# Block loads and accumulating additions pinned to program order on GpSimd's queue, the next set's first block asked for at product 2, gate halves spilled one set later

## The chip, the cores and the metric

The kernel runs on one core of a Trainium2 chip. The metric is the device time of one execution in microseconds. The core has a matrix engine (TensorE, PE in the profile), a vector engine (VectorE, DVE), a scalar engine (ScalarE, ACT), GpSimd (POOL) and a queue engine (SyncE, SP). SP and POOL issue DMA transfers, each from its own queue and in the order in which the instructions stand there; 16 DMA engines move the data.

## The reference, cut to what matters

One decoder layer: 256 tokens, width 2048, everything in float32. The change touches the middle of the combined input projection, where the gate columns are computed.

```
def reference(x, pre_norm_g, post_norm_g, w_in, ...):
    h = rmsnorm(x, pre_norm_g[l])
    proj = h @ w_in[l]
    (a_q, a_k, a_v, a_g, a_lr, b_q, b_k, b_v, b_g, m_a, m_b) = jnp.split(proj, offsets, axis=-1)
    ...
    o_a = rmsnorm(o_a, gla_norm_g[l]).reshape(B, S, GLA_VAL_DIM) * jax.nn.silu(a_g)
    o_b = o_b.reshape(B, S, DIFF_VAL_DIM) * jax.nn.silu(b_g)
    merged = jax.nn.sigmoid(m_a) * (o_a @ w_branch_a[l]) + jax.nn.sigmoid(m_b) * (o_b @ w_branch_b[l])
    return x + rmsnorm(merged @ w_out[l], post_norm_g[l])
```

## The kernel before

**Sets.** Weights are read from one packed array in device memory (`in_w_dram`). Eight sets of 1024 projection columns, numbered 0 to 7, and half a set, 8, are multiplied with a scheme of seven block products in place of eight. The columns of a set form a 2x2 arrangement of blocks, numbered 0 to 3, and each block is two tiles of 128x2048 (1 MB), t = 0 and 1, each used in two halves h. The products of a set run in the order `PRODUCTS = (1, 3, 5, 6, 2, 7, 4)` (L29). A product takes four halves, so a set takes 28; set 8 takes 14. "Product (5,1)" below is the second tile of product 5.

**What a product multiplies.** Two running tiles per t, called chain tiles, hold the operand. `a` starts as block 0 and is the operand of product 1; then block 1 is added to it in place by an accumulating DMA (`accumulate`, L254), and DVE adds `b` (L264), for products 5 and 6; later DVE adds block 2. `b` is block 3, the operand of product 3; block 1 is then added to it too, for product 7. Product 2 takes block 2 directly, from the tiles `c`. Product 4 uses `a` again. `link` (L229) loads a block into a chain tile; there are five such buffers, and four of them make one set. The tiles are called a, b and c in the profile; a0 and a1 below are the tiles for t = 0 and 1.

**Splitting.** Before PE multiplies a half, ACT rounds it to the fast matrix format (`hi`, L361) and DVE computes the remainder (`lo`, L362). `take` (L370) keeps these three halves ahead of PE (`AHEAD = 3`). PE multiplies hi with two parts of the input and lo with one: six matmuls of 512 columns per half, all in line L558 of the profile (a helper).

**Partners.** Between the halves of the sets PE runs halves of other projections (the last value columns, then k, q, dq and dk), one after each (product, t) listed in `PARTNERED` (L36): eight a set. `ALONE` (L38) takes one away from sets 2 and 5. Partner weights are the tiles `raw`, loaded by SP.

**When blocks are asked for.** `emit_set` (L235) runs when a half is split. At product (6,0) of a set it asks for the next set's a0, at (7,1) for a1, at (4,0) and (4,1) for b0 and b1. From set 1 on `link` puts these loads on POOL's queue, and `follow_set` (L251) puts the accumulating DMAs there, two halves per tile: a0 and a1 after their halves of product 1 are split, b0 and b1 after product (5,1) and (6,0).

**Gate halves.** Each set ends in two gate tiles of 128x1024 (512 KB), the right one `gr` (product 6 and 7) and the left one `gl` (product 2 and 4). ACT puts them through their activation, and `spill` (L181) writes them to device memory from POOL's queue: gr after product 7, gl after product 4 of the same set. They are fetched again far later. k, q, dq and dk (`dh`, `dl`) are spilled from POOL too. Gate halves, c, and the parts of k and q share 18 buffers (`u`, L165).

**Order.** A scheduler sets the order of the instructions of each engine, unless an instruction is held by `tc.keep_in_program_order`. The matmuls of this phase and all spills are held; the block loads and the accumulating DMAs are not.

Of the kernel before, what the change touches and what calls it, by code (L numbers as in the profile page):

```python
# [11 lines left out]
ALU = mybir.AluOpType  # L12
# [17 lines left out]
SETS = 8  # L30
# [3 lines left out]
LEAD = 6  # L34
EARLY = (0, 1)
PARTNERED = ((1, 1), (3, 1), (5, 1), (6, 0), (6, 1), (2, 1), (7, 0), (7, 1))  # L36
LAST_PARTNERED = (1, 3, 5, 6, 2, 7)
ALONE = ((2, 6, 1), (5, 6, 1))  # L38
BIG = 18
# [66 lines left out]
def phase_steps():  # L106
# [8 lines left out]
    for slot in slots:  # L115
        mixed += [("set", *slot, h) for h in range(2)]
        s, prod, t = slot
        with_partner = prod in LAST_PARTNERED if s == SETS else (prod, t) in PARTNERED and slot not in ALONE
        for _ in range(with_partner + (slot in front)):
# [30 lines left out]
def hybrid_kernel(ctx: ExitStack, tc, xt, xn, preg, postg, w, w2, gkb, glag, lamv, diffg, ident_d, causal_d, lmask_d, out):  # L150
    nc = tc.nc
    pe, act, dve, pool, sp = nc.tensor, nc.scalar, nc.vector, nc.gpsimd, nc.sync
# [12 lines left out]
    def u(shape, name, dtype=F32):  # L165
        count[0] += 1
        return big.tile(shape, dtype, tag="u", name=f"{name}_{count[0]}")
# [13 lines left out]
    def spill(t, name):  # L181
        count[0] += 1
        d = dram.tile(list(t.shape), t.dtype, name=f"{name}_{count[0]}")
        tc.keep_in_program_order(pool.dma_start(d, t))
        return d
# [34 lines left out]
    chain = {}  # L220

    def weights(key, r):
        a, size = at[key][r]
        return w[a : a + P * size].rearrange("(p n) -> p n", p=P), size

    def block(s, i, t):
        return weights(f"set{s}", i if s == SETS else 2 * i + t)[0]

    def link(s, name, t):  # L229
        count[0] += 1  # L230
        c = blocks.tile([P, 2048], F32, tag="chain", name=f"{name}_{count[0]}", bufs=5)
        (pool if s else sp).dma_start(c, block(s, {"a": 0, "b": 3}[name], t))
        chain[s, name, t] = c

    def emit_set(s, prod, t, h):  # L235
        c = slice(1024 * h, 1024 * h + 1024)
        few = 1 if s == SETS else 2
        name, i = {(6, 0): ("a", 0), (7, 1): ("a", 1), (4, 0): ("b", 0), (4, 1): ("b", 1)}.get((prod, t), (None, 0))
        if h == 0 and s < SETS and name and (i == 0 or s + 1 < SETS):
            link(s + 1, name, i)  # L240
        if h == 0 and s == 0 and prod == 1:
            link(s, "b", t)
        n = 2 * few * (PRODUCTS.index(prod) - PRODUCTS.index(2)) + 2 * t + h + LEAD
        if 0 <= n < 2 * few:
            i, j = n // 2, n % 2
            raws[s, i, j] = u([P, 1024], "c")
            sp.dma_start(raws[s, i, j], block(s, 2, i)[:, 1024 * j : 1024 * j + 1024])
        a, b = chain[s, "a", t], chain[s, "b", t]
        return raws[s, t, h] if prod == 2 else (b if prod in (3, 7) else a)[:, c]

    def follow_set(s, prod, t, h):  # L251
        c = slice(1024 * h, 1024 * h + 1024)

        def accumulate(name, i):  # L254
            pool.dma_start(chain[s, name, i][:, c], block(s, 1, i)[:, c], accum_op=ALU.add)  # L255

        if prod == 1:
            accumulate("a", t)
        steps = {(5, 0): 0, (2, 0): 0} if s == SETS else {(5, 1): 0, (6, 0): 1, (2, 1): 0, (7, 0): 1}
        i = steps.get((prod, t))  # L260
        if i is not None:
            a = chain[s, "a", i][:, c]
            second = prod in (5, 6)
            dve.tensor_tensor(out=a, in0=a, in1=chain[s, "b", i][:, c] if second else raws[s, i, h], op=ALU.add)  # L264
            if second:
                accumulate("b", i)
# [103 lines left out]
    def take(key):  # L370
        j = used[0]
        used[0] += 1
        while emitted[0] < min(j + 1 + AHEAD, len(seq)):
            emit_half()
        e, hi, lo = ready.pop(j)
        assert key in (e, e[0]), (e, key)
        return hi, lo
# [384 lines left out]
    gspill = [None] * (2 * SETS + 2)  # L762
# [62 lines left out]
    def operand(prod, kt):  # L825
# [2 lines left out]
            return [t[:, P * i : P * i + P] for t in x_ops(8 * j + kt)]  # L828
        return [t[:, kt, :] for t in sums[{3: "s4", 5: "r1", 6: "s2", 7: "r3"}[prod]]]

    def block_products(s):
        x = ps("mm")
        bank = {1: x, 6: x, 7: x, 4: x}
        kept, halves = {}, {}
        seeded = s > 0

        def right_done(b):
            dst = halves["r"][:, b, :]
            if s == SETS:
                return  # L840
            if s in MERGE:
                act.activation(dst, dst, AF.Tanh, scale=minus_half[:, b : b + 1])
            else:
                act.activation(dst, dst, AF.Silu, scale=minus_rstd[:, b : b + 1])

        def left_done(b, src):
            if s in MERGE:
                act.activation(halves["l"][:, b, :], src, AF.Tanh, scale=half_rstd[:, b : b + 1])
            elif s == GLA_GATES:
                gate(src, b, halves["l"][:, b, :])  # L850
            elif s < SETS:
                act.activation(halves["l"][:, b, :], src, AF.Copy, scale=rstd[:, b : b + 1])
            else:
                act.activation(halves["l"][:, b, :], src, AF.Copy)

        for prod in PRODUCTS:
            if prod not in bank:
                bank[prod] = ps("mm")
            out = bank[prod]
            few = 1 if s == SETS else 2  # L860
            for t in range(few):
                for h in range(2):
                    hi, lo = take(("set", s, prod, t, h))
                    for w, parts in ((hi, (0, 1)), (lo, (0,))):
                        for j in range(2):
                            kt = 4 * t + 2 * h + j
                            a = operand(prod, kt)
                            for part in parts:
                                first = prod not in ((6, 7, 2, 4) if seeded else (6, 7, 4)) and kt == 0 and w is hi and part == 0
                                last = kt == 4 * few - 1 and w is lo  # L870
                                i = mm(out, a[part], w[:, 512 * j : 512 * j + 512], start=first, stop=last, skip_group_check=out is x or prod == 2)
                    latest[0] = i.ins
                    if t == few - 1 and h:
                        if prod == 1 and seeded:
                            bank[2] = ps("mm")
                            act.activation(bank[2], x, AF.Copy)
                        elif prod in (1, 5):
                            kept[prod] = t2([P, 512], f"p{prod}")
                            act.activation(kept[prod], out, AF.Copy)
                        if prod == 5:  # L880
                            kept[3] = t2([P, 512], "p35")
                            dve.tensor_tensor(out=kept[3], in0=bank[3], in1=kept[5], op=ALU.add)
                        if prod == 6:
                            halves["r"] = u([P, 2, 512], "gr")
                            with tc.high_priority(offset=100):
                                dve.tensor_tensor(out=halves["r"][:, 0, :], in0=x, in1=kept[3], op=ALU.add)
                            right_done(0)
                        if prod == 2:
                            halves["l"] = u([P, 2, 512], "gl")
                            if not seeded:  # L890
                                dve.tensor_tensor(out=halves["l"][:, 0, :], in0=out, in1=kept[1], op=ALU.add)
                            left_done(0, out if seeded else halves["l"][:, 0, :])
                        if prod == 7:
                            with tc.high_priority(offset=100):
                                dve.tensor_tensor(out=halves["r"][:, 1, :], in0=x, in1=kept[5], op=ALU.add)
                            right_done(1)
                            gspill[2 * s + 1] = spill(halves["r"], "gr")
                        if prod == 4:
                            left_done(1, x)
                            gspill[2 * s] = spill(halves["l"], "gl")  # L900
                    yield

    sets = (step for s in range(SETS + 1) for step in block_products(s))
# [377 lines left out]
    for g in (2, 3):  # L1281
        parts = other_parts(2 * SETS) if g == 3 else None
        banks = token_major(f"ag{g}", 512, x_ops, LANES)
        t = u2([P, 2, 512], "ua")
# [283 lines left out]
    for g in (2, 3):  # L1568
# [7 lines left out]
        if g == 2:  # L1576
            total(0, 2, bank, 2)
            for b in range(2):
                xres.append([])
                for i in range(2):  # L1580
                    t = u([P, 1024], "xres")
# [3 lines left out]
    t = total(0, 3, bank)  # L1585
# [10 lines left out]
    for c in range(2):  # L1596
# [6 lines left out]
        if c == 0:  # L1603
            t = cell(1, 3)[:, :256]
# [4 lines left out]
        else:  # L1609
            end = ps("bg")  # L1610
            c = slice(TURNED[0] % 1024, TURNED[0] % 1024 + 512)
            t = yg[1, 1][:, c]
# [67 lines left out]
```

## Time and profile before

| | us |
|---|---|
| times of three runs | 1098.48, 1099.20, 1188.32 |
| median | 1099.20 |
| time of the profiled execution | 1101.01 |
| span of the profile | 1099.0 |
| sets 1 to 7, from product 3 of set 1 to product 3 of set 8 | 156.87 to 589.23 |

| engine | busy us in the span | share |
|---|---|---|
| PE | 1082.4 | 98% |
| DVE | 941.0 | 86% |
| ACT | 741.4 | 67% |
| POOL | 164.6 | 15% |

How to read it: the ends of pipelined matmuls are modelled, so a busy PE may still be late; what a set loses is read from the distance between the same matmul of two sets. A DMA has no row of its own for its duration: the timeline shows when its issue ran on its queue, and the view of DMA issues the median time from issue to landing. When an engine waits for a landing, its next instruction carries the idle time and the name of the DMA.

### The profile page before, as it was taken

What the parts mean: (1) busy time and instruction counts of PE and PEld (TensorE: products, weight loads), DVE (VectorE), ACT (ScalarE), POOL (GpSimd) and SP (SyncE); (2) the same over time, 40 slices, a digit from 0 to 9 for tenths busy, and PEclk for the clock granted to TensorE, in tenths of its full rate; (3) what the DMA queues carried; (4) which work ended last, traced back from release to release, by engine and by line L of the source; (5) the groups of instructions that cost most, each with busy time, mean ns of one, the idle gap of its engine ahead of it and who ended that gap; (6) DMA issues with size and microseconds to landing.
All of it is one profiled execution on the core that took longest, in us unless ns stands there. A gap on an engine that the chain in (4) does not pass through costs nothing.

```text
span 1099.0 us, 15379 instructions
## 1 busy us (share of the span) xinstructions
PE 1082.4 (98%) x5416; PEld 922.0 (84%) x5416; DVE 941.0 (86%) x1276; ACT 741.4 (67%) x1068; POOL 164.6 (15%) x245
## 2 busy tenths in 40 slices
PE   9999999999999999999999999999999999999997
PEld 8999887878787887888788888888888888888886
DVE  7788989898797979989898799986878878889886
ACT  7886776667566676767667676565677776566662
POOL 0211121212102121211202110012111011101000
PEclk9999999999999999999999999999999999999999
DMA  9899896987969898997968776689898898988752
GB/s 353 286 331 327 239 333 176 359 215 282 249 192 314 229 306 208 313 267 287 262 214 217 299 245 196 208 299 323 276 271 288 259 310 259 329 291 271 272 186 102
DMA packets 66669, 292.40 MB, mean 266 GB/s; under 512 B 8672, under 2 KB 11744, under 8 KB 49184
## 3 DMA queue, kind: packets, MB, share of 16 engines
q1 hardware_dynamic: 38944, 177.43, 45.8%
q0 software_dynamic: 27072, 113.26, 37.2%
q8 instruction: 42, 0.69, 0.2%
q10 hardware_dynamic: 576, 0.73, 0.2%
q14 instruction: 35, 0.29, 0.1%
HBM read 264.12 MB, written 27.26 MB: 265 GB/s over the span
## 4 chain that ended last, share of the span: by engine, by line
PE 79%; DMA 11%; DVE 5%; issue 3%; ACT 2%; POOL 1%; POOLq 0%; SPq 0%; ACTq 0%; DVEq 0%
PE mm L558 51%; PE bg L558 18%; DMA a<-in_w_dram 10%; DVE lo L362 3%; PE mm L546 2%; PE bg L546 2%; ACT hi L361 1%; DMA raw<-in_w_dram 1%; PE mm L531 1%; PE bg L986 1%; PE bg L531 1%; DVE a L264 1%; PE bg L1153 0%; PE bg L1127 0%; POOL a L255 0%
## 5 line engine op out<-in xcount | busy, mean ns | idle before, releaser
L361 ACT ACTIVATE hi<-raw 128x1024 fp32r<-128x1024 f32 (+3 forms) x237 | 243.1, 1029 | 158.4 <-PE mm L558 67.9
L362 DVE TENSOR_TENSOR lo<-raw,hi 128x1024 fp32r<-128x1024 f32 (+3 forms) x239 | 281.1, 1181 | 44.0 <-ACT hi L361 40.9
L362 DVE TENSOR_TENSOR lo<-a,hi 128x1024 fp32r<-128x1024 f32 x136 | 164.2, 1220 | 31.4 <-ACT hi L361 29.4
L361 ACT ACTIVATE hi<-a 128x1024 fp32r<-128x1024 f32 x136 | 143.2, 1058 | 69.8 <-PE mm L558 30.1
L558 PE MATMUL mm<-hi,xs 128*128 128x512 f32 (+1 forms) x728 | 184.5, 384 | 0.0
L558 PEld LDWEIGHTS mm<-hi,xs 128*128 128x128 f32 x728 | 135.5, 188 | 22.6
L558 PE MATMUL bg<-xs,hi 128*128 128x512 f32 x512 | 133.0, 392 | 0.0
L558 PEld LDWEIGHTS bg<-xs,hi 128*128 128x128 f32 x512 | 97.2, 190 | 19.4
L558 PE MATMUL mm<-lo,xs 128*128 128x512 f32 (+1 forms) x364 | 103.5, 383 | 1.1 <-DVE lo L362 1.1
L362 DVE TENSOR_TENSOR lo<-b,hi 128x1024 fp32r<-128x1024 f32 x68 | 82.6, 1220 | 16.4 <-ACT hi L361 14.3
L361 ACT ACTIVATE hi<-b 128x1024 fp32r<-128x1024 f32 x68 | 72.1, 1060 | 24.6 <-PE mm L558 16.4
L558 PEld LDWEIGHTS mm<-lo,xs 128*128 128x128 f32 x364 | 68.0, 188 | 14.2 <-DVE lo L362 2.4
L558 PEld LDWEIGHTS bg<-xs,lo 128*128 128x128 f32 x512 | 69.6, 190 | 6.8 <-DVE lo L362 2.1
L558 PE MATMUL bg<-xs,lo 128*128 128x256 f32 x512 | 71.7, 283 | 0.9 <-DVE lo L362 0.9
L558 PE MATMUL mm<-xs,hi 128*128 128x512 f32 x256 | 68.0, 397 | 0.0
L255 POOL DMA_DIRECT2D b<-in_w_dram x34 | 29.4, 863 | 167.8 <-DVE a L264 117.7
L558 PEld LDWEIGHTS mm<-xs,hi 128*128 128x128 f32 x256 | 46.1, 189 | 7.8
L558 PE MATMUL mm<-hi,oah 128*128 128x512 f32 x128 | 50.8, 397 | 0.0
L558 PE MATMUL mm<-hi,oal 128*128 128x512 f32 x128 | 50.0, 391 | 0.0
L361 ACT ACTIVATE hi<-c 128x1024 fp32r<-128x1024 f32 x34 | 36.1, 1060 | 14.1 <-PE mm L558 7.1
L264 DVE TENSOR_TENSOR a<-a,b 128x1024 f32<-128x1024 f32 x34 | 41.5, 1221 | 0.4
L264 DVE TENSOR_TENSOR a<-a,c 128x1024 f32<-128x1024 f32 x34 | 41.2, 1217 | 0.0
(419 smaller groups left out, 2178.6 us busy)
## 6 DMA issues: line engine op xcount, KB each, us to landing
raw<-in_w_dram SPq DMA_DIRECT2D x102, 1024.0 KB, 6.9
c<-in_w_dram SPq DMA_DIRECT2D x34, 512.0 KB, 9.5
a<-in_w_dram POOLq DMA_DIRECT2D x34, 512.0 KB, 12.5
b<-in_w_dram POOLq DMA_DIRECT2D x34, 512.0 KB, 7.0
a<-in_w_dram POOLq DMA_DIRECT2D x15, 1024.0 KB, 8.3
b<-in_w_dram POOLq DMA_DIRECT2D x15, 1024.0 KB, 9.4
raw<-in_w_dram SPq DMA_DIRECT2D x14, 832.0 KB, 6.8
gr<-gr POOLq DMA_DIRECT2D x9, 512.0 KB, 7.1
```

The lines of the kernel that those rows point to most:

```text
L255: pool.dma_start(chain[s, name, i][:, c], block(s, 1, i)[:, c], accum_op=ALU.add)
L264: dve.tensor_tensor(out=a, in0=a, in1=chain[s, "b", i][:, c] if second else raws[s, i, h], op=ALU.add)
L361: act.activation(hi_t[:, a:b], r[:, a:b], AF.Copy)
L362: dve.tensor_tensor(out=lo_t[:, a:b], in0=r[:, a:b], in1=f32(hi_t[:, a:b]), op=ALU.subtract)
L531: i = pe.matmul(out, lhs, rhs, start=first and n == 0, stop=last and n == len(pairs) - 1, **kw)
L546: i = pe.matmul(banks[g][b][:, :n], a[part][:, P * b : P * b + P], w[:, n * g : n * g + n], start=first, stop=last)
L558: i = pe.matmul(*args, **kw)
L986: pe.matmul(o, xk[:, P * c : P * c + P], xq.rearrange("p (b c t) -> p b c t", b=2, c=4)[:, :, c, :], start=i == 0, stop=i == 1)
```

## The change

Four edits, each in the phase of the sets:

1. The block loads of `link` and the accumulating DMAs of `accumulate` are held in program order, as the spills are. All of this work on POOL then stands as the program wrote it.
2. The next set's a0 is asked for at product (2,0), the fifth product, in place of (6,0), the fourth.
3. Both gate halves of a set are no longer spilled at its products 7 and 4. They are noted in a list, and the list is spilled just before the next set's product (6,0) is taken (`SPILL_AT`); those of set 8 are spilled at its end.
4. Through edit 1, SP's loads for set 0 (a0, a1, b0, b1) are held as well.

```diff
+SPILL_AT = (6, 0, 0)
...
     def link(s, name, t):
         count[0] += 1
         c = blocks.tile([P, 2048], F32, tag="chain", name=f"{name}_{count[0]}", bufs=5)
-        (pool if s else sp).dma_start(c, block(s, {"a": 0, "b": 3}[name], t))
+        tc.keep_in_program_order((pool if s else sp).dma_start(c, block(s, {"a": 0, "b": 3}[name], t)))
         chain[s, name, t] = c
...
-        name, i = {(6, 0): ("a", 0), (7, 1): ("a", 1), (4, 0): ("b", 0), (4, 1): ("b", 1)}.get((prod, t), (None, 0))
+        name, i = {(2, 0): ("a", 0), (7, 1): ("a", 1), (4, 0): ("b", 0), (4, 1): ("b", 1)}.get((prod, t), (None, 0))
...
-            pool.dma_start(chain[s, name, i][:, c], block(s, 1, i)[:, c], accum_op=ALU.add)
+            tc.keep_in_program_order(pool.dma_start(chain[s, name, i][:, c], block(s, 1, i)[:, c], accum_op=ALU.add))
...
+    owed = []
+
+    def settle_owed():
+        while owed:
+            n, t, name = owed.pop(0)
+            gspill[n] = spill(t, name)
+
     def block_products(s):
...
+                    if (prod, t, h) == SPILL_AT:
+                        settle_owed()
                     hi, lo = take(("set", s, prod, t, h))
...
                             right_done(1)
-                            gspill[2 * s + 1] = spill(halves["r"], "gr")
+                            owed.append((2 * s + 1, halves["r"], "gr"))
                         if prod == 4:
                             left_done(1, x)
-                            gspill[2 * s] = spill(halves["l"], "gl")
+                            owed.append((2 * s, halves["l"], "gl"))
+                            if s == SETS:
+                                settle_owed()
```

In the built programs this moves instructions as follows. The first place is POOL's queue where set 2 ends and set 3 begins (254 to 274 us of the trace). Loads have 2048 columns, accumulating DMAs 1024; spills name the tile on both sides. Before:

```order
L232 DMA a_2414<-in_w_dram 128x2048
L232 DMA b_2461<-in_w_dram 128x2048
L184 DMA gr_2485<-gr_2342 128x1024
L232 DMA b_2488<-in_w_dram 128x2048
L232 DMA a_2716<-in_w_dram 128x2048
L255 DMA a_2222<-in_w_dram 128x1024 x2
L255 DMA a_2414<-in_w_dram 128x1024
L184 DMA gl_2554<-gl_2390 128x1024
L255 DMA a_2414<-in_w_dram 128x1024
L255 DMA b_2461<-in_w_dram 128x1024 x2
L255 DMA b_2488<-in_w_dram 128x1024 x2
```

These are set 3's a1, b0 and b1, set 2's gr among them, then set 4's a0 (a_2716), and only then the accumulating DMAs of set 3, with set 2's gl ahead of the last one for a. Now:

```order
L233 DMA a_2414<-in_w_dram 128x2048
L233 DMA b_2461<-in_w_dram 128x2048
L233 DMA b_2486<-in_w_dram 128x2048
L256 DMA a_2295<-in_w_dram 128x1024 x2
L256 DMA a_2414<-in_w_dram 128x1024 x2
L256 DMA b_2461<-in_w_dram 128x1024 x2
L256 DMA b_2486<-in_w_dram 128x1024 x2
L185 DMA gr_2769<-gr_2342 128x1024
L185 DMA gl_2771<-gl_2390 128x1024
L233 DMA a_2814<-in_w_dram 128x2048
```

The two spills of set 2 and the load of set 4's a0 (now a_2814) moved from ahead of set 3's accumulating DMAs to behind all eight of them.

The second place is the same queue where set 6 ends (505 to 520 us of the trace); a_4490 and the two b are set 7's, dh and dl the split halves of a dk tile, gr_4558 set 6's, a_4798 set 8's a0. Before:

```order
L232 DMA a_4490<-in_w_dram 128x2048
L232 DMA b_4534<-in_w_dram 128x2048
L184 DMA dh_4486<-dh_4483 128x512
L184 DMA dl_4488<-dk_4301 128x512
L184 DMA gr_4558<-gr_4388 128x1024
L232 DMA b_4560<-in_w_dram 128x2048
L232 DMA a_4798<-in_w_dram 128x2048
```

Now, with a_4366 for set 7's a0 and gr_4317, gl_4319 for set 5's gate halves:

```order
L185 DMA gr_4317<-gr_3879 128x1024
L185 DMA gl_4319<-gl_3927 128x1024
L233 DMA a_4366<-in_w_dram 128x2048
L185 DMA dh_4486<-dh_4483 128x512
L185 DMA dl_4488<-dk_4295 128x512
L233 DMA a_4490<-in_w_dram 128x2048
L233 DMA b_4534<-in_w_dram 128x2048
L233 DMA b_4558<-in_w_dram 128x2048
```

Set 7's a1 (a_4490) and b0 moved from ahead of the spills dh and dl to behind them; the same holds one set earlier.

The third place is ACT at the end of product 2 of set 1 (about 192 us), with what each instruction waits for. Before:

```order
L361 ACTIVATE hi_1864<-raw_1770 128x1024 [waits DVE_49,PE_49]
L361 ACTIVATE hi_1874<-b_1446 128x1024 [waits DMASW3_49,DVE_49,PE_49]
L361 ACTIVATE hi_1887<-b_1446 128x1024 [waits DMASW4_49,DVE_49,PE_49]
L848 ACTIVATE gl_1898<-mm_1587,half_rstd 128x512 [waits PE_49]
L361 ACTIVATE hi_1900<-raw_1885 128x1024 [waits DMAHW2_49,DVE_49,PE_49]
```

Now:

```order
L362 ACTIVATE hi_1864<-raw_1768 128x1024 [waits DVE_49,PE_49]
L362 ACTIVATE hi_1874<-b_1446 128x1024 [waits DMASW0_49,DVE_49,PE_49]
L362 ACTIVATE hi_1887<-b_1446 128x1024 [waits DMASW1_49,DVE_49,PE_49]
L856 ACTIVATE gl_1898<-mm_1583,half_rstd 128x512 [waits DMASW4_49,PE_49]
L362 ACTIVATE hi_1900<-raw_1885 128x1024 [waits DMAHW2_49,DVE_49,PE_49]
```

The first write of set 1's gl now also waits for a POOL transfer, `DMASW4`: the spill of set 0's gr, whose buffer it takes over. The same wait stands in sets 2, 3 and 4.

## The prediction

> **What bounds the kernel now.** I read the page first, then the stretch of sets 1 to 7 alone, then what PE waited for in it, then the chain, then POOL and ACT around one place of the chain.
>
> ```profile
> PE 1082.4 (98%) x5416; PEld 922.0 (84%) x5416; DVE 941.0 (86%) x1276; ACT 741.4 (67%) x1068; POOL 164.6 (15%) x245
> 156.87:589.23 432.36, 423.81 (x2030) 351.79 (x2029) 383.17 (x370) 293.43 (x325) 77.23 (x109) 0.99 0.85 256
> 288.00:300.00 12.00, 9.83 (x38) 7.19 (x37) 10.49 (x10) 6.14 (x7) 2.59 (x3) 0.86 0.89 213
> 354.00:366.00 12.00, 10.17 (x40) 7.61 (x39) 10.48 (x11) 6.63 (x9) 3.22 (x4) 0.86 0.94 216
> ```
>
> PE is busy nearly throughout, so only what the sets lose beside pure PE work can be won. In the stretch from product 3 of set 1 to product 3 of set 8 (length, then busy time of PE, PEld, DVE, ACT, POOL, then the granted clock), PE idles 432.36 - 423.81 = 8.6 us, and in two 12 us pieces of it the clock is 0.86, which costs 2 x 12 x 0.14 = 3.4 us more.
>
> ```profile
> PE mm L558 <- ACT hi L361: 6.2, 6, 1.8
> PE mm L558 <- DVE lo L362: 1.1, 3, 0.4
> PE bg L558 <- DVE lo L362: 0.9, 2, 0.5
> ```
>
> Of PE's waits in that stretch 6.2 us end with ACT's rounding, 2.0 us with DVE's remainder. What is lost in all follows from the distance of equal matmuls:
>
> ```profile
> 156.87 0.40 PE L558 MATMUL mm<-hi,s4h 128*128 128x512 f32 x1
> 589.23 0.40 PE L558 MATMUL mm<-hi,s4h 128*128 128x512 f32 x1
> ...
> 185.76 5.47 PE mm L558 x24
> 191.23 2.77 PE bg L558 x16
> ```
>
> Four undisturbed set halves take 5.47 us, one partner 2.77. A set is 28 halves and 8 partners: 28 x 5.47 / 4 + 8 x 2.77 = 60.5 us. Seven such, less one partner in sets 2 and 5 and two halves of set 8's short product 1, are 423.2 - 5.5 - 2.7 = 415.0; the stretch has 432.4, so about 17 us are lost. Idle time and clock make 12.0 of it; the other 5 are gaps that modelled matmul ends cover.
>
> ```profile
> 270.91 21.26 DMA a<-in_w_dram x2
> ...
> 286.05 1.06 ACT L361 ACTIVATE hi<-a 128x1024 fp32r<-128x1024 f32 x1 [2.69 <-DMA a<-in_w_dram]
> 288.54 1.06 ACT L361 ACTIVATE hi<-a 128x1024 fp32r<-128x1024 f32 x1 [1.43 <-DMA a<-in_w_dram]
> 292.28 1.06 ACT L361 ACTIVATE hi<-a 128x1024 fp32r<-128x1024 f32 x1 [2.68 <-DMA a<-in_w_dram]
> ```
>
> The chain names the cause: a DMA into `a` stands in it for 21 us, and ACT sat idle for each half of product 5 until an addition had landed. These are the accumulating DMAs of set 3. POOL's issues just before:
>
> ```profile
> 264.87 0.54 POOL L184 DMA_DIRECT2D gr<-gr  x1 [5.39 <-ACT gr L844]
> 265.39 0.54 POOL L232 DMA_DIRECT2D b<-in_w_dram  x1
> 268.25 0.54 POOL L232 DMA_DIRECT2D a<-in_w_dram  x1 [2.31 <-DVE lo L362]
> 269.55 0.88 POOL L255 DMA_DIRECT2D a<-in_w_dram  x1 [0.77 <-DVE lo L362]
> 272.81 0.88 POOL L184 DMA_DIRECT2D gl<-gl  x1
> 273.97 0.86 POOL L255 DMA_DIRECT2D a<-in_w_dram  x1 [0.28 <-issue]
> ```
>
> and the landing of the issues at 264.87, 265.39, 268.25, 272.81 and 273.97, each taken alone:
>
> ```profile
> gr<-gr POOLq DMA_DIRECT2D x1, 512.0 KB, 7.1
> b<-in_w_dram POOLq DMA_DIRECT2D x1, 1024.0 KB, 9.3
> a<-in_w_dram POOLq DMA_DIRECT2D x1, 1024.0 KB, 8.9
> gl<-gl POOLq DMA_DIRECT2D x1, 512.0 KB, 16.9
> a<-in_w_dram POOLq DMA_DIRECT2D x1, 512.0 KB, 18.2
> ```
>
> They land in the order of issue: 272.0, 274.7, 277.2, 289.7, 292.2. An addition that directly follows another takes 288.54 - 286.05 = 2.5 us; set 4's a0 took 277.2 - 274.7 = 2.5, gl 289.7 - 288.5 = 1.2, gr (half a load) about 1.3. So 5.0 us of transfers that nobody needs soon stand before the last addition.
>
> **The change part by part.** *The load of a0 and both spills leave this place.* The four additions for a then come right behind b1, and the last of them lands 5.0 us sooner, near 287 in set 3. It had held (5,1,1), whose rounding began at 292.28. The split works three halves ahead, and PE idled at most 1.8 us at a time, so 5 us more than empties the wait. I take all 6.2 us of ACT-ended waits as won, the 3.4 us of clock, which lie right behind the two longest stalls, and the 5 us of covered gaps; of the waits that DVE ended I take nothing: 17 - 2.0 = 15.0 won. Below, only waits and clock are won, 9.6; above, all 17.
>
> *The same transfers come later,* behind the additions for b: 2 MB on POOL, about 5 us, while product 2 runs. Cover: from the start of product 2 (185.76 in set 1) products 2, 7 and 4 are 12 halves and 3 partners, 16.4 + 8.3 = 24.7 us, to the next use of an a0, against 8.9 us for its load to land. Cost 0; without that cover, each us late is a us of PE.
>
> *a1 moves behind dh and dl in sets 5 and 6.* In the trace of set 6, with the first use of a1 in ACT:
>
> ```profile
> 505.54 0.57 POOL L232 DMA_DIRECT2D a<-in_w_dram  x1 [16.88 <-DVE lo L362]
> ...
> 512.48 0.55 POOL L184 DMA_DIRECT2D dl<-dk  x1 [0.33 <-DVE dk L783]
> ...
> 520.55 1.06 ACT L361 ACTIVATE hi<-a 128x1024 fp32r<-128x1024 f32 x1 [0.30 <-DVE lo L362]
> ```
>
> The load would be issued at 513.0 in place of 505.5. It took 8.9 us to land, as the load at 268.25 did, and would be there at 521.9, 1.4 late for ACT. The a1 of a set earlier, issued at 444.75, took longer:
>
> ```profile
> a<-in_w_dram POOLq DMA_DIRECT2D x1, 1024.0 KB, 10.2
> ```
>
> With 10.2 it is 2.7 late. What queues behind: ACT's next roundings, b0 and b1 on POOL, the additions. From 0 (the lead of three halves hides it) to 2.7 each; I take 1.0 each, 2.0 in all.
>
> *gl waits for the spill of gr* in sets 1 to 4. In set 1 (POOL's last addition for b, that addition's landing, ACT's gl):
>
> ```profile
> 177.55 0.86 POOL L255 DMA_DIRECT2D b<-in_w_dram  x1 [1.07 <-ACT hi L361]
> b<-in_w_dram POOLq DMA_DIRECT2D x1, 512.0 KB, 9.3
> 191.78 0.67 ACT L848 ACTIVATE gl<-mm,half_rstd 128x512 f32<-128x512 f32 x1
> ```
>
> The addition lands at 186.9, gr 1.3 later at 188.2, 3.6 us before ACT needs the buffer. Cost 0; gone wrong, ACT's queue stands, and the splits behind it. SP's held loads of set 0 end in a part where PE idles nowhere:
>
> ```profile
> 60.00:120.00 60.00, 60.00 (x303) 55.91 (x302) 53.19 (x58) 45.05 (x58) 9.66 (x13) 1.00 1.00 311
> ```
>
> Cost 0, hidden by PE's work on the first projections; a load that came late there would show at once as idling.
>
> **Sum.** Won 15.0, lost 2.0: 13.0 us. The profiled execution took 1101.0 for a span of 1099.0 and would take 1088.0. The median of the runs is 1099.2, 1.8 lower, and I predict it: 1099.2 - 13.0 = 1086.2 us, 1.2% less.
>
> **Rivals.** *Half of it.* Another tail ahead of the additions takes over: b1 itself, issued late, and SP's loads. For it speaks the end of set 5, where the next a0 already stood behind the last addition:
>
> ```profile
> 463.03 0.86 POOL L255 DMA_DIRECT2D a<-in_w_dram  x1
> 463.58 0.87 POOL L232 DMA_DIRECT2D a<-in_w_dram  x1
> ...
> 463.03 15.42 DMA a<-in_w_dram
> ```
>
> and yet the addition needed 15.4 us. Then only the spills count, 2.5 of the 5.0 us, and half of the 15.0 is won: 1099.2 - 7.5 + 2.0 = 1093.7. Against it: dh, dl and late block loads crowd that place, not those of sets 1 to 4.
>
> *The change does not do what it says.* If SP's loads fill the room that is freed, the additions land no sooner: 1099. [...] Against it, from 148 to 153 us, before the additions of set 1:
>
> ```profile
> q0 software_dynamic: 280, 1.97, 100.7%
> q1 hardware_dynamic: 3, 0.02, 0.8%
> ```
>
> POOL's queue (q0) has the engines to itself, and SP (q1) moves nothing; it waits for buffers.
>
> *The half clock stays.* If the two dips to 0.86 have another cause than the stalls beside them, their 3.4 us stay lost: 1089.6. Against it, both lie right behind the longest waits for an addition, with 12.00 - 9.83 = 2.2 and 12.00 - 10.17 = 1.8 us of idling in the piece, and no other piece of the sets shows one. [...]
>
> *Slower: ACT stands at gl.* If gr's spill lands as slowly as gl did at 272.81, 16.9 us after an issue at 178.4, it is there at 195.3, 3.5 us after ACT wants it, and such a stall brings a clock dip of 1.7 us as at 288. In four sets that is 20.8 us against the 13.0 won: 1107. It decides from 13.0 / 4 - 1.7 = 1.6 us late per set, or 5.2 us more than I work out. Against it: at 178 us the queue ahead is two additions, not seven transfers.
>
> **How the numbers follow.** Forecast 0.65 (1086), clock stays 0.06 (1090), half 0.17 (1094), no effect 0.07 (1099), slower 0.05 (1107). The forecast's own bounds are 1099.2 - 17.0 = 1082.2 and 1099.2 - 9.6 + 5.4 = 1095.0. The range is 1081.5 to 1096.0: it takes in both bounds, the clock and the half case, and leaves out the last two and a little on either side. Over 2% (22 us) is about what a measurement of this kernel can tell from no change. Faster by that would need more than the 17 us that the sets lose: 0.03. Slower by that needs gl (22 + 13) / 4 - 1.7 = 7 us late in each set: 0.02. Within: 0.95.
>
> **What would show it.** Right: POOL's four additions for a follow b1 without another transfer, the last one for a lands 5 us sooner against product 3, ACT's waits for `DMA a` at product 5 vanish, PE's waits for ACT in the sets fall from 6.2 to under 1.5 us, and no stretch of the sets has a clock under 0.95. A distance between two sets' first s4h matmuls near 60.5 us (57.8 in sets 2 and 5) confirms the 17. Wrong: ACT idle before gl on `DMA gr`, idle before the first hi of a1 in sets 6 and 7 of more than 2 us, or the loss found again at product 2 or 7 with DVE as the releaser.

## The result, and the profile after

| | before | after |
|---|---|---|
| median of four runs | 1100.56 us | 1087.67 us |
| range | 1098.48 to 1101.91 and one of 1188.32 | 1087.25 to 1088.37 |
| profiled execution, its span | 1101.01, 1099.0 us | 1087.73, 1086.0 us |

The changed kernel takes 0.989 of the time before, with a 95% interval of 0.9869 to 0.9911; the run of 1188.32 us, like one of 2188.65 us of the kernel "no pins" below, is left out as a run in a slower state, and without it the median before is 1099.20 us. The forecast was 1086.2 us in a range of 1081.5 to 1096.0. The spans of the two profiled executions fell by 13.0 us, which is the forecast's sum; how they came to it is another matter, shown below. Between the medians of 1099.20 and 1087.67 us the fall is 11.5 us, since the execution profiled before stood 1.8 us above its median and the one profiled after only 0.1.

The busy line of the page after, and then the stretch from product 3 of set 1 to product 3 of set 8 with the two pieces that held the low clock before (length, busy time of PE, PEld, DVE, ACT, POOL, then granted clock, DMA share, GB/s):

```profile
PE 1075.1 (99%) x5416; PEld 920.2 (85%) x5416; DVE 939.7 (87%) x1276; ACT 742.1 (68%) x1068; POOL 164.0 (15%) x245
```

```profile
159.30:574.86 415.56, 415.15 (x2030) 350.97 (x2029) 381.92 (x370) 294.70 (x325) 77.50 (x110) 1.00 0.91 267
288.00:300.00 12.00, 12.00 (x61) 10.22 (x60) 12.00 (x14) 8.21 (x10) 4.62 (x7) 1.00 0.95 215
354.00:366.00 12.00, 12.00 (x66) 10.40 (x65) 12.00 (x14) 7.26 (x8) 2.79 (x5) 1.00 1.03 278
```

The stretch took 432.36 us and takes 415.56; the prediction's count of undisturbed halves and partners gave 415.0. PE idles 0.4 us in it where it idled 8.6, and the clock is full. What PE still waits for there, in total, times and longest:

```profile
PE mm L559 <- DVE lo L363: 0.4, 1, 0.4
```

The waits that ended with ACT, 6.2 us, are gone, and of the 2.0 us that ended with DVE 0.4 are left. The cause on POOL, the same place in set 3 as shown of before, where the load of b1 and the additions for a are issued:

```profile
265.61 0.54 POOL L233 DMA_DIRECT2D b<-in_w_dram  x1 [5.96 <-DVE lo L363]
269.59 0.88 POOL L256 DMA_DIRECT2D a<-in_w_dram  x1 [3.44 <-DVE lo L363]
270.95 0.86 POOL L256 DMA_DIRECT2D a<-in_w_dram  x1 [0.48 <-DVE lo L363]
272.30 0.86 POOL L256 DMA_DIRECT2D a<-in_w_dram  x1 [0.48 <-DVE lo L363]
273.82 0.85 POOL L256 DMA_DIRECT2D a<-in_w_dram  x1 [0.67 <-DVE lo L363]
```

Nothing stands between b1 and the four additions now. The landing of the last of them, taken alone, and ACT's rounding of the last two halves of product 5:

```profile
a<-in_w_dram POOLq DMA_DIRECT2D x1, 512.0 KB, 13.4
```

```profile
285.63 1.06 ACT L362 ACTIVATE hi<-a 128x1024 fp32r<-128x1024 f32 x1 [1.20 <-PE bg L559]
287.51 1.06 ACT L362 ACTIVATE hi<-a 128x1024 fp32r<-128x1024 f32 x1 [0.82 <-PE mm L559]
```

It lands at 273.82 + 13.4 = 287.2 in place of 292.2. Set 3 begins at 278.1 us in both executions, so this is the 5.0 us of the forecast. ACT no longer waits for the addition but for PE to free the buffer it writes to; the idle time before its rounding ends with PE, which is what an unhindered split looks like.

So 16.8 us were won in the sets, and only 13.0 arrived. The other 3.8 lie ahead of the sets and behind them. `s4h` is the part of the input that only product 3 multiplies in the sets, so the first s4h matmul of a set marks its start here, and its distance to that of the next set is the set's length. For set 0, before, and then after with four more rows of PE:

```profile
93.71 0.40 PE L558 MATMUL mm<-hi,s4h 128*128 128x512 f32 x1
```

```profile
54.29 0.46 PE L559 MATMUL mm<-hi,xs 128*128 128x416 f32 x1 [0.38 <-ACT hi L362]
78.69 0.46 PE L559 MATMUL mm<-lo,xs 128*128 128x416 f32 x1 [0.42 <-DVE lo L363]
96.15 0.40 PE L559 MATMUL mm<-hi,s4h 128*128 128x512 f32 x1
574.86 0.40 PE L559 MATMUL mm<-hi,s4h 128*128 128x512 f32 x1
634.39 0.50 PE L991 MATMUL bg<-atl,ones_r 128*128 128x512 f32 x1 [0.92 <-DVE atl L977]
```

Set 0 begins 2.4 us later, with two waits before it, of 0.38 and 0.42 us, that before did not have. From product 3 of set 8 to the end it was 1099.0 - 589.23 = 509.8 us and is 1086.0 - 574.86 = 511.1, 1.4 more, with one new wait of 0.92 us for `atl`, a tile that DVE writes. Thus 16.8 - 2.4 - 1.4 = 13.0.

### The profile page after: what moved, and what is told of

Read it like the earlier page. It is cut to its first block, busy times and chain, and to the rows that moved or that the text cites. A ratio compares the mean times of both kernels' runs of the same rounds, so it can differ in the third digit from the quotient of the medians.

```text
span 1086.0 us, 15356 instructions
## 1 busy us (share of the span) xinstructions
PE 1075.1 (99%) x5416; PEld 920.2 (85%) x5416; DVE 939.7 (87%) x1276; ACT 742.1 (68%) x1068; POOL 164.0 (15%) x245
## 4 chain that ended last, share of the span: by engine, by line
PE 91%; DVE 3%; ACT 3%; issue 2%; DMA 1%; POOL 0%; POOLq 0%; SPq 0%; ACTq 0%; DVEq 0%
PE mm L559 58%; PE bg L559 23%; PE mm L547 2%; PE bg L547 2%; DMA raw<-in_w_dram 1%; DVE lo L363 1%; PE mm L532 1%; PE bg L998 1%; ACT hi L362 1%; PE bg L532 1%; PE bg L1165 0%; PE bg L1139 0%; PE bg L1140 0%; PE bg L1177 0%; PE bg L1178 0%
## 5 line engine op out<-in xcount | busy, mean ns | idle before, releaser
L559 PEld LDWEIGHTS bg<-xs,hi 128*128 128x128 f32 x512 | 96.2, 188 | 18.7
```

Of the source, the lines that this page charges most:

```text
L559: i = pe.matmul(*args, **kw)
```

## The experiments

Three numbers are read from each profile: the start of set 0 (first s4h matmul), the stretch as above, and what lies behind it. "Ahead" is the length of transfers on POOL's queue ahead of the last addition for a that the changed kernel does not have there, by the durations of the prediction (a0 2.5 us, gr 1.3, gl 1.2). The first three numbers are of the one profiled execution, the time is the median of the runs compared; the profiled execution of "gl ahead", "a0 ahead", "pins alone" and "spills after additions" was the fastest of its runs, 1.2 to 1.9 us under the median, that of "both ahead" the slowest, 1.2 above. Before the change the 5.0 us hold for sets 1 to 5 and 7 only: in set 6 the next a0 stood behind the additions already. Ratios below are against runs of the kernel before on the same chip, whose medians lay between 1099.2 and 1100.2 us.

| kernel | ahead | start of set 0 | stretch | behind | time, median |
|---|---|---|---|---|---|
| before | 5.0 | 93.7 | 432.4 | 509.8 | 1099.2 |
| after | 0 | 96.2 | 415.6 | 511.1 | 1087.7 |
| gl ahead | 1.2 | 95.6 | 417.0 | 510.5 | 1089.3 |
| a0 ahead | 2.5 | 96.0 | 420.8 | 510.4 | 1094.0 |
| spills ahead | 2.5 | 96.0 | 423.1 | 509.8 | 1093.6 |
| both ahead | 5.0 | 95.7 | 441.8 | 511.1 | 1112.6 |
| both, a1 free | 5.0 | 95.8 | 435.4 | 510.5 | 1107.3 |
| pins alone | 2.5 | 95.5 | 421.8 | 509.8 | 1093.9 |
| no pins | 2.5 | 93.0 | 417.7 | 512.7 | 1088.1 |
| spills after a0 | 0 | 95.9 | 415.6 | 510.9 | 1087.6 |
| front free | 0 | 93.8 | 415.5 | 511.9 | 1086.2 |
| front and last | 0 | 93.3 | 416.0 | 510.0 | 1084.6 |
| spills after additions | 0 | 93.0 | 415.5 | 511.0 | 1085.6 |

### Putting the transfers back, in pinned order

Three theories run through the next three expectations. A: transfers ahead of the additions set the time. B: the fixed order as such made the gain. C: only the spills count. "Both ahead" makes two edits, the place of a0 and the two spills, which are also made alone, as "a0 ahead" and "spills ahead":

```diff
-        name, i = {(2, 0): ("a", 0), (7, 1): ...
+        name, i = {(1, 0): ("a", 0), (7, 1): ...
...
-                            owed.append((2 * s + 1, halves["r"], "gr"))
+                            gspill[2 * s + 1] = spill(halves["r"], "gr")
...
-                            owed.append((2 * s, halves["l"], "gl"))
+                            gspill[2 * s] = spill(halves["l"], "gl")
```

> The changed kernel, all pins kept, with a0 asked at the first product and gr and gl spilled at once: 5.0 us of transfers ahead of the last addition, as before the change, in a pinned order. Theory A: 5.0 less 1.9 us to spare is 3.1 us a set in the sets where nothing else hides it, with clock dips behind the longest stalls: 1100 to 1105, about 17 us more than the changed kernel. Theory B: 1087.7. Theory C: as with the spills alone. The last half of product 5 waits for a DMA into a again, and PE for ACT.

1112.61 us (1110.8 to 1113.81), 1.0115 of the time before, 1.0095 to 1.0134. That is 8 us above what theory A had at most, so A's size is missed. The pins are all there, and the loss is back: an order that is merely fixed wins nothing, so theory B falls. ACT in set 3 of this kernel reads as before the change:

```profile
287.86 1.06 ACT L362 ACTIVATE hi<-a 128x1024 fp32r<-128x1024 f32 x1 [2.86 <-DMA a<-in_w_dram]
290.35 1.06 ACT L362 ACTIVATE hi<-a 128x1024 fp32r<-128x1024 f32 x1 [1.43 <-DMA a<-in_w_dram]
294.08 1.06 ACT L362 ACTIVATE hi<-a 128x1024 fp32r<-128x1024 f32 x1 [2.68 <-DMA a<-in_w_dram]
```

and PE waits for ACT longer than before:

```profile
PE mm L559 <- ACT hi L362: 11.9, 8, 3.5
```

The distances from one set's first s4h matmul to the next's, for sets 1 to 7, say where. Before: 61.66, 59.59, 65.07, 64.54, 59.62, 61.65, 60.23. Both ahead: 61.61, 59.66, 64.93, 64.74, 59.41, 66.67, 64.79. After: 60.43, 58.42, 60.43, 60.43, 57.72, 60.42, 57.71. In sets 1 to 5 the kernel before is reproduced to 0.2 us a set. Sets 6 and 7 lose 9.6 us more than before; no theory had that.

> The changed kernel with the next set's a0 asked at the first product, so that its 1 MB load stands on POOL ahead of all four additions for a, pinned there; spills stay late. Theory A (transfers ahead of the additions set the time): 2.5 of the 5.0 us are back. In the changed kernel the last half of product 5 is rounded at 287.51 to 288.57 and PE wants it at 290.49, so 1.9 us are spare: a loss of about 0.6 us a set and little more, 1089 to 1093. Theory B (the order as such, or fewer waits for semaphores, made the gain): no loss, 1087.7. Theory C (half of it: only the spills counted): 1087.7 as well.

1093.99 us (1092.09 to 1096.58), ratio 0.9955, 0.994 to 0.997: a loss of 5.3 us in the stretch, and a median 1.0 us above theory A's range. B and C, both 1087.7, are out.

> The changed kernel with gr and gl spilled as soon as they are there, as before the change, ahead of the last addition for a; a0 stays at product 2. Theory A: 2.5 us of transfers are back ahead of the last addition against 1.9 us to spare, so 1089 to 1093. Theory B (pinned order made the gain): 1087.7. Theory C (only the spills counted): the whole loss of the sets is back, 1100 to 1104.

1093.64 us (1092.82 to 1093.89), ratio 0.9947, 0.9932 to 0.9961: 7.6 us in the stretch, not the 16.8 of theory C. The two halves cost 5.3 and 7.6 alone and 16.8 to 26.3 together. Part of the 26.3 are the 9.6 us of sets 6 and 7; in sets 1 to 5 alone it is 2.1 and 2.9 us alone against 12.9 together. That speaks for a threshold and not for a proportion, and gl alone tests it:

```diff
-                            owed.append((2 * s, halves["l"], "gl"))
+                            gspill[2 * s] = spill(halves["l"], "gl")
```

> The changed kernel with gl alone spilled as soon as it is there, ahead of the last addition for a: 1.2 us of transfer against the 1.9 us that ACT has to spare there in set 3. Theory A, a threshold: what fits into the spare time costs nothing, so 1087 to 1088.5 and 415.6 to 416.5 us for the stretch of sets 1 to 7. Theory F, in proportion: 1.2 / 2.5 of the 7.6 us that both spills cost, 3.6 us: 1091.

1089.31 us (1088.09 to 1090.93), ratio 0.9905, 0.9887 to 0.9923; the stretch is 1.4 us longer. Median and stretch, 417.0 us, lie between the two theories, above the 1088.5 and 416.5 that A allowed, and the sets tell the theories apart: their distances are those of the changed kernel within 0.25 us but for set 6, with 61.65 for 60.42. Set 3 gives the cleanest series: 60.43 with nothing ahead, 60.43 with 1.2 us, 60.61 and 61.32 with 2.5, 64.93 and (before) 65.07 with 5.0. The 1.9 us to spare that were read off ACT's and PE's rows fit that: "both, a1 free" below, with 5.0 us ahead and no dip of the clock in set 3, has 63.66, which is 3.2 more than nothing ahead, where 5.0 - 1.9 is 3.1. The threshold is not the same in every set. Sets 1 and 2 lose nothing with 2.5 us, while set 4 loses 0.24 us with 1.2 and 1.9 to 2.0 with 2.5. In set 6 the rows read as for set 3 give 1.6 us to spare, and there the last addition lands at 467.6 us with gl ahead and at 464.8 in the changed kernel.

### One part of the change alone

The pins alone, on the kernel before:

```diff
-        (pool if s else sp).dma_start(c, block(...))
+        tc.keep_in_program_order((pool if s else sp).dma_start(c, block(...)))
...
-            pool.dma_start(chain[...], block(...), accum_op=ALU.add)
+            tc.keep_in_program_order(pool.dma_start(chain[...], block(...), accum_op=ALU.add))
```

> The kernel before with the pins alone: block loads and additions in program order on POOL, a0 still asked at product 6 and gr and gl spilled at once. In program order a0 then falls between the additions for b, so it leaves the additions for a; both spills stay ahead of the last of them. Theory A (transfers ahead of the additions for a set the time): as with the spills ahead, 423 us for the stretch of sets 1 to 7 instead of 432, and a little for a0 ahead of the additions for b: 1092 to 1097. If the place of a0 among the additions for b matters as much, PE waits before product 7 and the gain is gone: 1099.

1093.9 us (1092.04 to 1095.65), ratio 0.9946, 0.9926 to 0.9967, and 421.8 us for the stretch. Pinned, a0 falls between the additions for b, where it costs no more than behind them all: the stretch of "spills ahead", where it stands there, has 423.1 us.

The same pins undone on the changed kernel, which leaves the late spills and the other place for a0:

> The changed kernel without any pin on loads and additions: the scheduler puts a0 ahead of the additions for a again and leaves the loads of set 0 early; spills stay late. Theory A: the stretch of sets 1 to 7 as with a0 asked at the first product, 421 us, and the front 2.3 us shorter than in the changed kernel: 1089 to 1092. If pins cost or gain something of their own in sets 6 and 7, where the program order puts dh and dl ahead of a1, the difference shows there and nowhere else.

1088.1 us, the median of three runs (1085.53 to 1088.41), ratio 0.9887, 0.9864 to 0.991. POOL in set 3:

```profile
262.76 0.54 POOL L233 DMA_DIRECT2D b<-in_w_dram  x1 [6.10 <-DVE lo L363]
265.43 0.54 POOL L233 DMA_DIRECT2D a<-in_w_dram  x1 [2.13 <-DVE lo L363]
266.74 0.88 POOL L256 DMA_DIRECT2D a<-in_w_dram  x1 [0.77 <-DVE lo L363]
```

The scheduler puts the next a0 (line 233) right ahead of the additions (line 256) here, as it did before the change, though the program now asks for it a product later: in this set the second edit does nothing without the first. Yet the late spills alone win 432.4 - 417.7 = 14.6 us of the 16.8 in the stretch. The place of a0 and the pins on POOL add 2.2, and the pins on SP take 2.4 at the front. Sets 6 and 7 are undisturbed here, 60.43 and 57.70 us, where "a0 ahead", with a0 at the same place but pinned, has 63.05 and 58.24: the pins do cost something there. Without them a1 of set 6 stands ahead of dh on POOL (433.23 us) and b0 between dh and dl, as before the change; pinned, both stand behind dl (442.56).

### Sets 6 and 7

In "both ahead", a1's load is pinned behind dh and dl; before, the scheduler had it ahead of them (b0 too in set 6; in set 5 b0 stood between dh and dl). The load of a1 alone is left free:

```diff
-        tc.keep_in_program_order((pool if s else sp).dma_start(c, block(...)))
+        i = (pool if s else sp).dma_start(c, block(...))
+        if (name, t) != ("a", 1) or not s:
+            tc.keep_in_program_order(i)
```

> The kernel with 5.0 us of transfers ahead of the additions in pinned order (1112.6 us, 13 more than before the change), with the loads of a1 alone left to the scheduler, which puts them ahead of dh and dl in sets 5 and 6 again, as before the change. Theory G (the pinned place of a1 behind dh and dl costs, once the spare time is used up): the distance of the first s4h matmuls of set 7 falls from 64.8 to about 60.2, as before the change, that of set 6 from 66.7 to 62 to 64, in all 5 to 9 us: 1103 to 1108. If pins as such cost it (waits, order on ACT), nothing changes: 1112.

1107.3 us (1106.24 to 1108.01), ratio 1.0063, 1.0047 to 1.0079. POOL at the end of set 6, with both ahead and with a1 free:

```profile
517.78 0.58 POOL L185 DMA_DIRECT2D dh<-dh  x1 [22.78 <-ACT dh L783]
519.57 0.57 POOL L185 DMA_DIRECT2D dl<-dk  x1 [1.22 <-DVE dk L784]
```

```profile
510.66 0.57 POOL L233 DMA_DIRECT2D a<-in_w_dram  x1 [18.39 <-DVE lo L365]
516.16 0.55 POOL L233 DMA_DIRECT2D b<-in_w_dram  x1 [4.94 <-DVE lo L365]
516.71 0.56 POOL L185 DMA_DIRECT2D dh<-dh  x1
```

With a1 at 510.66 the distance of set 7 is 60.18, as before the change (60.23), in place of 64.79: G holds there. The pinned b0 moves ahead of dh along with a1 (516.16), so the 4.6 us are the price of both loads standing behind dh, for which POOL stands 22.78 us, when nothing is to spare. The distance of set 6 stays at 66.46, where 62 to 64 was expected. On POOL the place that still differs from before there is the next a0, which stood behind the last addition for a at the end of set 5 and stands ahead of it here. That this makes the other 4.8 us was not tried alone; "spills ahead" and "both ahead", whose edits differ in the place of a0 alone, have 63.45 and 66.67 us in set 6, so 3.2 us of it can be put down to a0 there.

### The transfers that were put off

```diff
-SPILL_AT = (6, 0, 0)
+SPILL_AT = (2, 0, 0)
```

> The changed kernel with gr and gl of the set before spilled later still, at product 2, so that on POOL they stand behind the load of a0 and behind a spill of q or k where there is one: gr lands about 2.5 to 3.7 us later. In the changed kernel it lands 3.6 us ahead of ACT's gl in set 1, 2.2 in set 2, 6.0 in set 3, 2.9 to 5.9 after that. Theory A: ACT stands at gl for 0.1 us in set 1, for 1.5 in set 2 and hardly elsewhere, and the lead of three halves hides most of it: 1087.7 to 1090. The rival of the forecast (a stall of ACT at gl costs its length and a clock dip of 1.7 us): 1091 and more.

1087.59 us (1086.89 to 1088.56), ratio 0.989, 0.9872 to 0.9907: no cost that shows. In set 1 gr is issued here, with the landing of that issue taken alone,

```profile
186.69 0.54 POOL L185 DMA_DIRECT2D gr<-gr  x1
```

```profile
gr<-gr POOLq DMA_DIRECT2D x1, 512.0 KB, 8.5
```

and lands at 195.2, yet ACT writes gl ahead of that:

```profile
192.68 0.67 ACT L856 ACTIVATE gl<-mm,half_rstd 128x512 f32<-128x512 f32 x1
```

So gl must lie in another buffer in set 1 of this kernel, and the wait that the rival needs is not there. The run shows that the late transfers are free during product 2; it does not test what a stall of ACT at gl would cost, which stays open. In the changed kernel itself, where gl does wait for that buffer, POOL's issue, its landing and ACT's gl in set 1 are:

```profile
179.04 0.66 POOL L185 DMA_DIRECT2D gr<-gr  x1
...
192.97 0.67 ACT L856 ACTIVATE gl<-mm,half_rstd 128x512 f32<-128x512 f32 x1
```

```profile
gr<-gr POOLq DMA_DIRECT2D x1, 512.0 KB, 10.4
```

It lands at 189.4, 3.6 us ahead of gl.

Earlier is as good for the sets. With both ends mended (next part) and `SPILL_AT = (3, 0, 0)`:

> The kernel of the run before with both ends mended (loads of set 0 free, last gr spilled at once; 1084.6 us), with gr and gl of the set before spilled at product 3 instead of product 6: right behind the last addition for a, ahead of the additions for b. Theory A (only what stands ahead of the last addition for a costs): the spills land about 2.5 us behind it, at 287, before the first addition for b is even issued at 284.7 and due 5 to 6 us later: the sets stay at 416 us and the time at 1084 to 1085.5. If any transfer near the additions costs, the stretch of sets 1 to 7 is 2 to 8 us longer: 1087 and more.

1085.64 us (1084.44 to 1086.27), ratio 0.9866, 0.985 to 0.9881. POOL in set 3, with both spills right behind the last addition for a:

```profile
270.67 0.85 POOL L258 DMA_DIRECT2D a<-in_w_dram  x1 [0.66 <-DVE lo L365]
271.22 0.87 POOL L185 DMA_DIRECT2D gr<-gr  x1
271.77 0.86 POOL L185 DMA_DIRECT2D gl<-gl  x1
284.62 0.90 POOL L258 DMA_DIRECT2D b<-in_w_dram  x1 [11.99 <-DVE a L267]
```

The stretch is 415.5 us. Behind the last addition and the two spills POOL issues nothing for 12 us: that room is free. The part behind the sets is 1.0 us longer than in "front and last", and the time 1.1.

### The two ends

Where does SP ask for a0 of set 0? Before, and after:

```profile
19.72 0.42 SPq L232 DMA_DIRECT2D a<-in_w_dram  x1
```

```profile
44.29 1.69 SPq L233 DMA_DIRECT2D a<-in_w_dram  x2
52.41 15.31 SPq L313 DMA_DIRECT2D raw<-in_w_dram  x4
```

Pinned, a0 and a1 go out together at 44.29, among the loads of `raw` that the first projections read. Yet no row of PE, ACT or DVE from 38 to 96 us waits for a load in either kernel. What differs is the order on DVE. Before, and then after, with the row of ACT that follows from it (`rstd_bc` is a copy that waits for a matmul, `vl` the remainder of the value columns):

```profile
44.08 1.18 DVE L681 SCALAR_TENSOR_TENSOR vl<-mm,rstd,vh 128x400 fp32r<-128x400 f32 x2
46.66 0.42 DVE L489 COPY rstd_bc<-bg 128x256 f32<-128x256 f32 x1 [0.92 <-PE bg L488]
```

```profile
46.51 0.42 DVE L490 COPY rstd_bc<-bg 128x256 f32<-128x256 f32 x1 [2.63 <-PE bg L489]
46.85 1.17 DVE L682 SCALAR_TENSOR_TENSOR vl<-mm,rstd,vh 128x400 fp32r<-128x400 f32 x2
47.52 0.44 ACT L694 ACTIVATE lr<-mm,rstd 128x16 f32<-128x16 f32 x2 [2.64 <-DVE vl L682]
```

The copy stands ahead of `vl` now, DVE stands 2.63 us for it, ACT 2.64 us for `vl`, and the roundings behind come late. The program does not ask for this order; the scheduler chose it. The pin undone for set 0 alone:

```diff
+        i = (pool if s else sp).dma_start(c, block(...))
+        if s:
+            tc.keep_in_program_order(i)
```

> The changed kernel, but the block loads of set 0 on SP's queue are left to the scheduler (only those of sets 1 to 8 are pinned). Theory A: the pin on set 0 is what puts the first s4h matmul at 96.15 instead of 93.71 us; free, the front is back at 93.7 and the time falls by 2.4 us, from 1087.7 to about 1085.3. Theory B: the front is late because additions and loads for set 1 moved on POOL, which this kernel leaves as they are; then the time stays at 1087.7 and the first s4h matmul at 96.1.

1086.22 us (1085.46 to 1087.05), ratio 0.9881, 0.9866 to 0.9895. Set 0 begins at 93.80: theory A. The seven other kernels that pin the loads of set 0 begin it at 95.5 to 96.0 us, the four that leave them free at 93.0 to 93.8. All eight that pin have the copy ahead of `vl` and the two waits of about 0.4 us, and all five that do not, the kernel before among them, have it behind the first `vl` and no such wait. The 2.4 us lie at the two waits: from 44 to 60 us PE starts 84 matmuls where it started 92, from 70 to 80 us 49 where it started 55, and as many as before from 60 to 70 and from 80 to 92; at 10 us for 55 matmuls, 14 missing ones are about 2.5 us (an estimate). Why the scheduler changes DVE's order when loads of SP are held was not followed. The time fell by 1.5 and not 2.4 us, since the part behind the sets is 511.9.

For that part, gr of set 8 spilled at once, on top of the free front:

```diff
                             owed.append((2 * s + 1, halves["r"], "gr"))
+                            if s == SETS:
+                                settle_owed()
```

> The changed kernel with the loads of set 0 left to the scheduler and, in set 8, gr spilled as soon as it is there instead of after gl. Theory D: behind the sets the changed kernel loses 1.4 to 2.1 us since gr of set 8 is spilled 34.5 us after that set's first s4h matmul instead of 26.4, and DVE stands 4.3 us at xq for its buffer, which makes PE wait 0.9 us for atl; spilled at once, that wait goes and the part behind the sets is back at 509.8 us: with the front about 1084. Theory E: that part is longer because other instructions moved on DVE and ACT; then it stays at 511 to 512 and the time at 1086.

1084.56 us (1083.26 to 1085.03), ratio 0.986, 0.9839 to 0.9881. POOL's spill of that gr, and all that PE waits for after the start of set 1:

```profile
598.92 0.54 POOL L185 DMA_DIRECT2D gr<-gr  x1 [9.11 <-DVE gr L907]
```

```profile
PE bg L1634 <- ACT diag L1633: 1.0, 1, 1.0
PE mm L561 <- DVE lo L365: 0.6, 2, 0.4
```

The spill stands 598.92 - 572.52 = 26.4 us behind that set's first s4h matmul, as before the change, the wait for atl is gone (in the changed kernel DVE stands 4.34 us for the landing of that spill at 616.61 us, ahead of atl), and the part behind the sets takes 510.0 us: theory D for this kernel. It is not the whole: kernels that spill gr of set 8 late need 510.4 to 512.7 us there, those that spill it at once 509.8 to 511.1, so about 1 us hangs on the order of other instructions. This version beats the changed kernel by 3.1 us between medians, and its slowest run is under the other's fastest.

## Why the prediction was right

**The cause holds.** The 5.0 us of transfers are what stood ahead of the last addition: it lands 5.0 us sooner, ACT's waits there vanish, and putting the transfers back under pins gives sets 1 to 5 of the kernel before again. What the same transfers cost beyond that in set 6 is open in part.

**Won, 15.0 forecast, 16.8 measured.** The waits that DVE ended, 2.0 us kept as a loss, went as well, all but 0.4, with the late additions: they were no bound of DVE. Set 2 came out at 58.42 us and not at the 57.8 of the forecast's sign; that is the 0.6 us by which the stretch misses 415.0, and its cause stays open.

**a1 behind dh and dl, 2.0 forecast, 0 measured.** The working had a1 1.4 to 2.7 us late for ACT in each of the two sets, and took 1.0 of each as a loss of PE. After, at the end of set 5:

```profile
449.01 1.06 ACT L362 ACTIVATE hi<-a 128x1024 fp32r<-128x1024 f32 x1 [1.04 <-DMA a<-in_w_dram]
```

ACT stands 1.04 us for a1 of set 6 and not at all for that of set 7, so the lateness was taken too large, and the lead of three halves hides what is left from PE. The last experiment on sets 6 and 7 shows the price when that lead is spent: 4.6 us in one set.

**Late transfers and gl, 0 forecast, 0 measured.** The margin at gl in set 1 came out at 3.6 us, the number forecast, though gr landed 1.2 us later than worked out (189.4 for 188.2): ACT's gl came 1.2 us later too, since the set began 2.4 us later.

**SP's held loads of set 0, 0 forecast, 2.4 us measured.** This step failed. It argued that PE idled nowhere from 60 to 120 us, so that a late load would be hidden, and looked at loads only. No load came late for PE, ACT or DVE. The hold came with another order on DVE, a wait of 2.63 us there and of 2.64 us on ACT, and a part in which PE never idles has no spare time to give for that. **Behind the sets**, the forecast had no term, and 1.4 us were lost: 0.92 in the wait for atl, which goes with the late spill of set 8's gr, the rest within what the order of other instructions moves there. The two errors, 3.8 us together, cancel the 3.8 us that the sets gave beyond the 13.0: the mechanism in the sets was right, but that the sum met the spans to 0.1 us was luck.

**Rivals.** Half: its premise, that the spills alone count, is wrong in the form given; spills removed alone win 14.6 us of 16.8, since what is left then nearly fits the spare time. Clock: gone with the stalls, 1.00 in both pieces that had 0.86. No effect: SP's loads did not fill the room, for the last addition for a in set 3 landed at 287.2 us in place of 292.2. Slower: not seen; no run made ACT stand at gl, so the price of that stays open.

## What to carry to other kernels

In this kernel a transfer ahead of a needed one cost not its length but about its length less the spare time at the place where the result is used (3.2 us in set 3 for 5.0 us of transfers and 1.9 to spare); so a0 and the two spills, which cost 5.3 and 7.6 us of the stretch alone, cost 16.8 to 26.3 together, and removing one of the two alone won most of the 16.8: 9.3 without a0 there ("spills ahead"), 14.6 with the spills late ("no pins"). Count the spare time first, from the landing to the row in which the waiting engine wants the data, and put what nobody waits for right behind the urgent transfers. A hold on the order of loads should cover only the stage that needs it: here the hold on four loads of SP at the start of the kernel cost 2.4 us, though none of them came late, because the scheduler then ordered another engine's instructions otherwise. After adding a hold, compare the order on every engine, not only on the held queue.

## What the runs showed of the chip

The clock does not always fall after the same wait. Stretches of 8 us around a wait of PE of 1.74 us with both ahead, and around one of 1.73 us with a1 free:

```profile
292.00:300.00 8.00, 6.20 (x20) 4.30 (x19) 6.63 (x7) 4.50 (x5) 1.57 (x2) 0.79 0.89 173
```

```profile
292.00:300.00 8.00, 6.14 (x28) 4.26 (x28) 6.63 (x6) 4.39 (x5) 1.74 (x2) 1.00 0.87 165
```

PE was busy about equally long in both, 6.20 and 6.14 us, and the clock is 0.79 in one and 1.00 in the other. Of five waits of 1.73 to 1.79 us in the sets, three stand in 8 us with a clock of 0.79 (1.74 and 1.76 us before the change, 1.74 with both ahead) and two in 8 us with 1.00 (1.73 and 1.79 us with a1 free). Around a wait of 3.08 us with a1 free the clock is 0.64 from 480 to 488 us; around one of 1.11 us before the change it is 1.00 from 540 to 548 us. With both ahead, where PE's longest wait is 3.5 us, it is 0.62 from 552 to 560 us. A dip of 0.79 over 8 us is 8 x 0.21 = 1.7 us lost, an estimate from the clock alone.
